# Moving the weight sums of a seven-product matrix multiplication into accumulating transfers, and scaling its inputs once

## The chip, the cores and the metric

The kernel runs on one NeuronCore of a Trainium2 chip. Its engines work from their own in-order queues: PE (TensorE, matrix multiplication), DVE (VectorE) and ACT (ScalarE) for element-wise work, POOL (GpSimd) for slower element-wise work, SP (SyncE), which here issues most DMA transfers. Sixteen DMA engines move the data. The metric is the time of one execution on the device in microseconds; lower is better. Three runs of the kernel before took 2226.47 to 2231.89 us, with a median of 2231.1.

## The reference, cut to what matters

One layer of a streaming encoder over 512 positions and 2048 channels, in float32. The change lies in its second half, the convolutional feed-forward block:

```
h    = rms_norm(x, pre_ffn_g)                      # x: 512 x 2048
up   = causal_depthwise_conv(h @ w_up, conv_w)     # w_up: 2048 x 11264, conv of 3 taps
gate, val = split(up, 2)                           # 5632 channels each
f    = (gelu(gate) * val) @ w_down                 # w_down: 5632 x 2048
x    = x + rms_norm(f, post_ffn_g)
```

The norm's factor (called r2 below) is one number per position, so it can be multiplied to h before the matrix product or to the product after it.

## The kernel before, in words

Tensors lie transposed: channels on the 128 partitions, the 512 positions along the free dimension. For precision each float32 operand of a matrix product is split into a high part (ACT, a cast to float32r) and the rest (DVE, a subtraction); a product is three matmuls, high x high, high x low, low x high. For weights ACT's cast `wh` is on L787 and DVE's subtraction `wl` on L788 (L100 and L101 in the plain products).

The 44 blocks of 128 hidden channels (`f`) each have a gate half and a val half. The first NP = 4 blocks are computed in the plain way by `up(0)` and `up(1)`, two blocks each, with `gemm`. The other 40 are the rows that this text speaks of: the loop `for f in range(NP, NFF)`. In a row, the 2 x 2 block product of weights (gate/val x lower/upper half of the input channels: w11, w12, w21, w22) and inputs (input-channel halves x position halves: q11, q12, q21, q22) is formed with seven products of half size instead of eight, from sums of weight blocks and sums of input quarters. Each `product` is 24 matmuls of 256 columns on one PSUM tile. Order on PE in a row: w11 x "11"; then, by `quad_end`, the last two products of the previous row (w22 x "t4", w12 x "22"); then s1 x "t1", s1 x "t2", w12 x "21", and w21 x "t3". The products of "t3" read on the trace as matmuls with `t2h`, those of "t1" and "t2" with `t0h` and `t1h`, or the like, by tile number.

Before the rows, the sums of the input quarters are made (`xsum`, L757) and split (`xsplit`, L761 and L762) from h without r2, so every result of a row has to be multiplied by r2 afterwards: GpSimd does that on L819 (val) and L823 (gate). Of the weights, `quad_load` fetches all four blocks (L801 to L810) with SP's queue, and GpSimd makes w21 + w22 into s1 (L805) and w11 - w21 into w21's buffer (L808). DVE makes the two other sums in the row, s1 - w11 (L841) and w12 - s1 (L848). DVE also combines the products in PSUM into gate and val (L818, L822, L845, L853, L854). `gated` then does the three taps of the convolution (first tap ACT on L726, two DVE on L728), ACT's gelu (L731), the product of gate and val (GpSimd, L732), and SP stores the block in DRAM (`fscr`, L733).

After the rows `down` multiplies the hidden blocks by w_down, four blocks at a time. `fload` loads four stored blocks (L876) and splits them (ACT L878, DVE L880).

The program states priorities (`tc.high_priority`: WPRI for weights, EPRI for what leaves PSUM), and a scheduler writes each engine's order from them before the run. A tile has a number of buffers; a load into one waits until the last reader of its former content is through. Tiles of a closed pool pass their place on: the pool `sp` of the rows (weight sums, `rb`, and a third pair of split buffers) is opened after `s16` is closed, which held the input quarters `yo`, and `hid`, of `down`, after the rows' `xt`.

## Time and profile before

| what | value |
|---|---|
| runs | 2226.47, 2231.1, 2231.89 us (median 2231.1) |
| profiled execution, its own time | 2227.7 us |
| its span, first to last instruction | 2225.9 us |
| mean granted TensorE clock | 0.966 of full speed |
| rows (40) | about 770 to 1704 us of the span |
| `down` | from about 1718 us on |

A busy share is an engine's busy time over the span. Matmuls are pipelined: one is shown for 0.28 us while the next starts 0.12 us later, so starts are what to count. A line such as "L845 DVE TENSOR_TENSOR ab<-mm,ab" is line 845 of the kernel, its engine, its operation, and the tiles it writes and reads. What stands in brackets behind "idle before" is how long the engine waited and for whom. "wl<-rb", "wl<-wraw" and "wl<-s" are the same subtraction on weights from different buffers.

### The profile page before, as it was taken

To read this page: it belongs to the slowest core of one execution; us is meant where nothing else is said; L and a number is where in the kernel's file an instruction comes from. 1 tells how busy PE (TensorE), PEld (TensorE's weight loads), DVE (VectorE), ACT (ScalarE), POOL (GpSimd) and SP (SyncE) were. 2 spreads that over 40 slices of the span, in tenths; PEclk is the share of its full clock that TensorE was granted. 3 is DMA by queue.
4 is the path that set the end of the run, shared out by engine and by line. 5 is a ranking of instruction groups with operands and counts; after the bars stand their busy time and mean duration, and the time that the engine had idled before them with its cause. 6 is when DMAs were issued, how large, how long until landed. Compare 5 with 4: busy or idle time off the path is not lost.

```text
span 2225.9 us, 30245 instructions
## 1 busy us (share of the span) xinstructions
PE 1997.7 (90%) x12070; PEld 1761.6 (79%) x12070; DVE 1688.0 (76%) x1893; ACT 811.2 (36%) x1047; POOL 725.6 (33%) x493
## 2 busy tenths in 40 slices
PE   7777988999987999989898998989987999999995
PEld 6565876777876789888898898988886888888884
DVE  5398999996459688988988889888886355555545
ACT  5112234334555433443433444334334422222223
POOL 7564145212123344435444444454441000000004
PEclk9888998999999999999999999999998999999998
DMA  5765665222423323233232332322225333433322
GB/s 198 190 207 178 186 206 164 95 95 85 171 99 119 127 101 106 94 111 103 89 116 95 102 110 88 119 96 100 105 95 194 123 114 119 135 116 114 104 95 95
DMA packets 124077, 275.88 MB, mean 124 GB/s; under 512 B 29472, under 2 KB 50976, under 8 KB 123424
## 3 DMA queue, kind: packets, MB, share of 16 engines
q1 hardware_dynamic: 119184, 271.85, 37.0%
q10 hardware_dynamic: 4752, 2.11, 0.4%
q8 instruction: 94, 1.54, 0.3%
q14 instruction: 47, 0.39, 0.1%
HBM read 241.21 MB, written 32.70 MB: 123 GB/s over the span
## 4 chain that ended last, share of the span: by engine, by line
PE 37%; DVE 20%; issue 7%; ACT 3%; DMA 0%; ACTq 0%; DVEq 0%; SPq 0%
PE mm L120 8%; PE mm L122 8%; PE mm L121 8%; DVE wl L788 7%; PE mm L793 5%; PE mm L794 4%; PE mm L795 4%; DVE s L841 4%; ACT wh L787 3%; DVE tmp L728 3%; DVE wraw L848 3%; DVE ab L822 1%; DVE ab L845 1%; DMA fin<-fscr 0%; DVE fa L920 0%
## 5 line engine op out<-in xcount | busy, mean ns | idle before, releaser
L101 DVE TENSOR_TENSOR wl<-wraw,wh 128x1024 fp32r<-128x1024 f32 (+1 forms) x193 | 254.6, 1320 | 245.5 <-ACT wh L100 239.5
L100 ACT CAST wh<-wraw 128x1024 fp32r<-128x1024 f32 (+1 forms) x193 | 201.6, 1046 | 508.8 <-PE mm L121 458.3
L122 PE MATMUL mm<-hl,wl 128*128 128x512 f32 x832 | 316.0, 412 | 64.5 <-DVE wl L101 64.5
L793 PE MATMUL mm<-hl,wh 128*128 128x256 f32 x1280 | 366.1, 286 | 5.7 <-ACT wh L787 5.1
L795 PE MATMUL mm<-hl,wl 128*128 128x256 f32 x1280 | 362.2, 283 | 0.0
L794 PE MATMUL mm<-hl,wh 128*128 128x256 f32 x1280 | 362.1, 283 | 0.0
L120 PE MATMUL mm<-hl,wh 128*128 128x512 f32 x832 | 333.6, 405 | 20.6 <-ACT wh L100 12.5
L121 PE MATMUL mm<-hl,wh 128*128 128x512 f32 x832 | 332.7, 402 | 0.2 <-DVE hl L691 0.2
L120 PE MATMUL mm<-hidh,wh 128*128 128x512 f32 x704 | 274.9, 391 | 14.4 <-ACT hidh L878 14.4
L121 PE MATMUL mm<-hidl,wh 128*128 128x512 f32 x704 | 274.6, 390 | 0.0
L122 PE MATMUL mm<-hidh,wl 128*128 128x512 f32 x704 | 258.1, 390 | 0.0
L793 PEld LDWEIGHTS mm<-hl,wh 128*128 128x128 f32 x1280 | 245.6, 192 | 10.8 <-ACT wh L787 7.3
L122 PEld LDWEIGHTS mm<-hl,wl 128*128 128x128 f32 x832 | 164.4, 198 | 111.2 <-DVE wl L101 76.1
L795 PEld LDWEIGHTS mm<-hl,wl 128*128 128x128 f32 x1280 | 245.8, 192 | 0.0
L794 PEld LDWEIGHTS mm<-hl,wh 128*128 128x128 f32 x1280 | 245.7, 192 | 0.0
L788 DVE TENSOR_TENSOR wl<-s,wh 128x1024 fp32r<-128x1024 f32 x80 | 162.2, 2028 | 89.1 <-ACT wh L787 89.1
L120 PEld LDWEIGHTS mm<-hl,wh 128*128 128x128 f32 x832 | 163.1, 196 | 57.3 <-ACT wh L100 14.2
L788 DVE TENSOR_TENSOR wl<-wraw,wh 128x1024 fp32r<-128x1024 f32 x120 | 194.4, 1620 | 7.4 <-ACT wh L787 4.6
L121 PEld LDWEIGHTS mm<-hl,wh 128*128 128x128 f32 x832 | 162.3, 195 | 36.4 <-DVE hl L691 1.2
L787 ACT CAST wh<-s 128x1024 fp32r<-128x1024 f32 x80 | 83.8, 1048 | 281.0 <-DVE s L841 169.1
L805 POOL TENSOR_TENSOR s<-rb 128x1024 f32<-128x1024 f32 x40 | 106.1, 2653 | 231.1 <-DMA rb<-in_ffn_w_quad 231.1
L571 DVE SCALAR_TENSOR_TENSOR csb<-z,c_conv_w,csb 128x512 f32<-128x512 f32 x210 | 178.8, 907 | 2.0 <-ACT csb L564 1.9
(262 smaller groups left out, 4111.9 us busy)
## 6 DMA issues: line engine op xcount, KB each, us to landing
wraw<-in_ffn_w_down SPq DMA_DIRECT2D x88, 512.0 KB, 3.2
wraw<-in_ffn_w_quad SPq DMA_DIRECT2D x80, 512.0 KB, 3.3
rb<-in_ffn_w_quad SPq DMA_DIRECT2D x80, 512.0 KB, 3.3
wraw<-in_w_in SPq DMA_DIRECT2D x47, 512.0 KB, 4.7
wraw<-in_w_out SPq DMA_DIRECT2D x32, 512.0 KB, 3.2
fscr<-tmp SPq DMA_DIRECT2D x44, 256.0 KB, 2.0
fin<-fscr SPq DMA_DIRECT2D x44, 256.0 KB, 3.8
cst<-cscr SPq DMA_DIRECT2D x16, 576.0 KB, 4.2
```

The lines of the kernel that those rows point to most:

```text
L100: se.copy(out=h[:, o], in_=raw[:, o])
L101: ve.tensor_tensor(out=l[:, o], in0=raw[:, o], in1=h[:, o].bitcast(F32), op=SUB)
L120: pe.matmul(ps[m], wh[:, kk, m, :], xh, start=k == 0, stop=False)
L121: pe.matmul(ps[m], wh[:, kk, m, :], xl, start=False, stop=False)
L122: pe.matmul(ps[m], wl[:, kk, m, :], xh, start=False, stop=k == nk - 1)
L571: ve.scalar_tensor_tensor(out=csb[:, c, :], in0=zk, scalar=w, in1=csb[:, c, :], op0=MUL, op1=ADD)
L787: se.copy(out=h, in_=raw)
L788: ve.tensor_tensor(out=l, in0=raw, in1=h.bitcast(F32), op=SUB)
L793: pe.matmul(o, h[:, k, :], xh_[:, k, :], start=first and k == 0, stop=False, skip_group_check=True)
L794: pe.matmul(o, h[:, k, :], xl_[:, k, :], start=False, stop=False, skip_group_check=True)
L795: pe.matmul(o, l[:, k, :], xh_[:, k, :], start=False, stop=last and k == 7, skip_group_check=True)
L805: ge.tensor_tensor(out=s1, in0=w21, in1=w22, op=ADD)
```

## The change: what it does

Four things, in the rows and around them.

The input quarters are multiplied by r2 once, in place, after up(0); the sums are then of scaled quarters, and all seven inputs are split anew: "t1", "t2", "t3" before up(1), and "11", "21", "t4", "22" after it in program order. The products need no r2 afterwards, so L819 and L823 go. "22" is split with its sign changed, and signs change in the sums that follow.

s1 is made by a load of w21 and an accumulating transfer that adds w22 to it in place, and a new s3 by a load of w11 and an accumulating transfer that adds w21. Both accumulating transfers are issued by GpSimd. w11, w12 and w22 are loaded as before, so a row has five plain loads and two accumulating ones. `rb` has two buffers instead of four, s3 has two.

The product of gate and val moves from GpSimd to DVE. In the first row the product w11 x "11" goes behind the two with s1.

Before the last `quad_end`, the first four hidden blocks are loaded from DRAM into tiles that are free by then (`evt`, `um`), and `fload(0)` uses these.

```diff
--- before.py
+++ after.py
@@ -717,7 +717,7 @@
         na[0] += 1
         return t
 
-    def gated(f, ab, mul):
+    def gated(f, ab):
         cvt = []
         for j in range(2):
             c = f + NFF * j
@@ -729,7 +729,7 @@
                                         op0=MUL, op1=ADD)
             cvt.append(o)
         se.activation(out=cvt[0], in_=cvt[0], func=AF.Gelu_apprx_tanh)
-        mul.tensor_tensor(out=cvt[0], in0=cvt[0], in1=cvt[1], op=MUL)
+        ve.tensor_tensor(out=cvt[0], in0=cvt[0], in1=cvt[1], op=MUL)
         sy.dma_start(out=fscr[:, f, :], in_=cvt[0])
 
     def up(i):
@@ -741,11 +741,16 @@
                 ve.tensor_tensor(out=t[:, 2:], in0=ps[j], in1=r2, op=MUL)
             ab.append(t)
         for f in range(2):
-            gated(2 * i + f, ab[2 * f:2 * f + 2], ge)
+            gated(2 * i + f, ab[2 * f:2 * f + 2])
 
     up(0)
 
 
+    for i in range(2):
+        for j in range(2):
+            o = slice(HS * j, HS * j + HS)
+            ve.tensor_tensor(out=yo[i][:, :, o], in0=yo[i][:, :, o],
+                             in1=r2[:, o].unsqueeze(1).broadcast_to([P, 8, HS]), op=MUL)
     q11, q12 = yo[0][:, :, 0:HS], yo[0][:, :, HS:S]
     q21, q22 = yo[1][:, :, 0:HS], yo[1][:, :, HS:S]
     xset = {"11": (hh[0][:, :, 0:HS], hl_[0][:, :, 0:HS]), "21": (hh[1][:, :, 0:HS], hl_[1][:, :, 0:HS]),
@@ -753,24 +758,33 @@
     for i in range(3):
         xset[f"t{i + 1}"] = tuple(tset[i])
 
-    def xsum(name, dst, in0, in1):
+    def xsum(dst, in0, in1):
         ve.tensor_tensor(out=dst, in0=in0, in1=in1, op=SUB)
 
-    def xsplit(name, src):
+    def xsplit(name, src, sign=1.0):
         h, l = xset[name]
-        se.copy(out=h, in_=src)
-        ve.tensor_tensor(out=l, in0=src, in1=h.bitcast(F32), op=SUB)
-
-    xsum("t1", q11, q12, q11)
-    xsplit("t1", q11)
-    xsum("t3", q12, q22, q12)
-    xsum("t2", q22, q22, q11)
-    xsplit("t2", q22)
+        if sign > 0:
+            se.copy(out=h, in_=src)
+            ve.tensor_tensor(out=l, in0=src, in1=h.bitcast(F32), op=SUB)
+        else:
+            se.activation(out=h, in_=src, func=AF.Copy, scale=-1.0)
+            ve.scalar_tensor_tensor(out=l, in0=src, scalar=-1.0, in1=h.bitcast(F32), op0=MUL, op1=SUB)
+
+
+    xsum(q12, q12, q11)
+    xsplit("t1", q12)
+    xsum(q12, q22, q12)
+    xsplit("t2", q12)
+    xsum(q12, q11, q12)
     xsplit("t3", q12)
-    xsum("t4", q21, q21, q22)
+    xsum(q12, q12, q11)
+    ve.tensor_tensor(out=q12, in0=q12, in1=q21, op=ADD)
     for i in range(1, NP // 2):
         up(i)
-    xsplit("t4", q21)
+    xsplit("11", q11)
+    xsplit("21", q21)
+    xsplit("t4", q12)
+    xsplit("22", q22, -1.0)
     s16x.close()
 
 
@@ -797,62 +811,71 @@
     def quad_load(f):
         src = a["ffn_w_quad"][f - NP]
         with tc.high_priority(offset=WPRI):
-            w21 = sp.tile([P, 1024], F32, name="rb", bufs=4)
-            sy.dma_start(out=w21, in_=src[2])
-            w22 = sp.tile([P, 1024], F32, name="rb", bufs=4)
-            sy.dma_start(out=w22, in_=src[3])
             s1 = sp.tile([P, 1024], F32, name="s1", bufs=2)
-            ge.tensor_tensor(out=s1, in0=w21, in1=w22, op=ADD)
+            sy.dma_start(out=s1, in_=src[2])
+            s3 = sp.tile([P, 1024], F32, name="s3", bufs=2)
+            sy.dma_start(out=s3, in_=src[0])
             w11 = wp.tile([P, 1024], F32, name="wraw", bufs=3)
             sy.dma_start(out=w11, in_=src[0])
-            ge.tensor_tensor(out=w21, in0=w11, in1=w21, op=SUB)
+            ge.dma_start(out=s1, in_=src[3], accum_op=ADD)
+            ge.dma_start(out=s3, in_=src[2], accum_op=ADD)
             w12 = wp.tile([P, 1024], F32, name="wraw", bufs=3)
             sy.dma_start(out=w12, in_=src[1])
-        return w11, w12, w21, w22, s1
+            w22 = sp.tile([P, 1024], F32, name="rb", bufs=2)
+            sy.dma_start(out=w22, in_=src[3])
+        return w11, w12, s3, w22, s1
 
     def quad_end(f, st_):
-        (w11, w12, w21, w22, s1), ab, (px, py, pz) = st_
+        (w11, w12, s3, w22, s1), ab, (px, py, pz) = st_
         gate, val = ab
         product(w22, "t4", py, False, True)
         with tc.high_priority(offset=EPRI):
-            ve.tensor_tensor(out=val[:, 2:2 + HS], in0=py[:, 0:HS], in1=val[:, 2:2 + HS], op=ADD)
-            ge.tensor_tensor(out=val[:, 2:], in0=val[:, 2:], in1=r2, op=MUL)
+            ve.tensor_tensor(out=val[:, 2:2 + HS], in0=py[:, 0:HS], in1=val[:, 2:2 + HS], op=SUB)
         product(w12, "22", pz, False, True)
         with tc.high_priority(offset=EPRI):
-            ve.tensor_tensor(out=gate[:, 2 + HS:], in0=pz[:, 0:HS], in1=gate[:, 2 + HS:], op=ADD)
-            ge.tensor_tensor(out=gate[:, 2:], in0=gate[:, 2:], in1=r2, op=MUL)
-        gated(f, ab, ge)
+            ve.scalar_tensor_tensor(out=gate[:, 2 + HS:], in0=pz[:, 0:HS], scalar=-1.0, in1=gate[:, 2 + HS:],
+                                    op0=MUL, op1=SUB)
+        gated(f, ab)
 
     before = None
     for f in range(NP, NFF):
         ws = quad_load(f)
-        w11, w12, w21, w22, s1 = ws
+        w11, w12, s3, w22, s1 = ws
         ab = [anext(), anext()]
         gate, val = ab
-        px = psm.tile([P, S], F32, name="mm")
-        product(w11, "11", px, True, False)
-        with tc.high_priority(offset=EPRI):
-            se.copy(out=val[:, 2:2 + HS], in_=px[:, 0:HS])
+        px, pz, py = (psm.tile([P, S], F32, name="mm") for _ in range(3))
+
+        def p1():
+            product(w11, "11", px, True, False)
+            with tc.high_priority(offset=EPRI):
+                se.copy(out=val[:, 2:2 + HS], in_=px[:, 0:HS])
+
         if before:
+            p1()
             quad_end(f - 1, before)
-        pz = psm.tile([P, S], F32, name="mm")
         product(s1, "t1", pz, True, False)
         with tc.high_priority(offset=WPRI):
-            ve.tensor_tensor(out=s1, in0=s1, in1=w11, op=SUB)
-        py = psm.tile([P, S], F32, name="mm")
+            ve.tensor_tensor(out=s1, in0=s1, in1=w11, op=ADD)
         product(s1, "t2", py, True, False)
+        if not before:
+            p1()
         with tc.high_priority(offset=EPRI):
-            ve.tensor_tensor(out=gate[:, 2 + HS:], in0=py[:, 0:HS], in1=val[:, 2:2 + HS], op=ADD)
+            ve.tensor_tensor(out=gate[:, 2 + HS:], in0=py[:, 0:HS], in1=val[:, 2:2 + HS], op=SUB)
         product(w12, "21", px, False, True)
         with tc.high_priority(offset=WPRI):
-            ve.tensor_tensor(out=w12, in0=w12, in1=s1, op=SUB)
+            ve.tensor_tensor(out=w12, in0=w12, in1=s1, op=ADD)
         with tc.high_priority(offset=EPRI):
             se.copy(out=gate[:, 2:2 + HS], in_=px[:, 0:HS])
-        product(w21, "t3", py, False, False)
+        product(s3, "t3", py, False, False)
         with tc.high_priority(offset=EPRI):
-            ve.tensor_tensor(out=val[:, 2 + HS:], in0=py[:, 0:HS], in1=val[:, 2:2 + HS], op=ADD)
+            ve.tensor_tensor(out=val[:, 2 + HS:], in0=py[:, 0:HS], in1=val[:, 2:2 + HS], op=SUB)
             ve.tensor_tensor(out=val[:, 2 + HS:], in0=pz[:, 0:HS], in1=val[:, 2 + HS:], op=ADD)
         before = (ws, ab, (px, py, pz))
+    f0 = []
+    for i in range(4):
+        t = evt() if i < 2 else t1.tile([P, S], F32, name="um", bufs=2)
+        sy.dma_start(out=t, in_=fscr[:, i, :])
+        f0.append(t)
     quad_end(NFF - 1, before)
     spx.close()
     upx.close()
@@ -872,8 +895,11 @@
     def fload(b):
         r = []
         for i in range(4):
-            t = hid.tile([P, S], F32, name="fin", bufs=6)
-            sy.dma_start(out=t, in_=fscr[:, 4 * b + i, :])
+            if b:
+                t = hid.tile([P, S], F32, name="fin", bufs=6)
+                sy.dma_start(out=t, in_=fscr[:, 4 * b + i, :])
+            else:
+                t = f0[i]
             h = hid.tile([P, S], F32R, name="hidh")
             se.copy(out=h, in_=t)
             l = hid.tile([P, S], F32R, name="hidl")
```

## Rows read from the trace of the kernel before

**Rows 1.** The page, part 1: busy us, share of the span, instructions.
```profile
PE 1997.7 (90%) x12070; PEld 1761.6 (79%) x12070; DVE 1688.0 (76%) x1893; ACT 811.2 (36%) x1047; POOL 725.6 (33%) x493
```

**Rows 2.** Stretches: busy us (instructions) per engine, PEclk, DMA share, GB/s.
```profile
800.00:1690.00 890.00, 806.44 (x6400) 782.40 (x6401) 789.40 (x688) 357.00 (x459) 394.89 (x189) 0.99 0.30 101
1650.01:1673.68 23.67, 21.10 (x168) 20.38 (x168) 21.22 (x19) 9.32 (x12) 9.97 (x6) 1.00 0.30 99
1673.68:1693.72 20.04, 20.04 (x167) 20.00 (x167) 17.19 (x19) 8.34 (x10) 3.58 (x4) 1.00 0.19 66
```

**Rows 3.** PE timeline, one t3 start: start us, duration us, instruction, idle before.
```profile
1673.68 0.38 PE L793 MATMUL mm<-t2h,wh 128*128 128x256 f32 x1 [1.44 <-DVE ab L845]
```

**Rows 4.** Single lines of DVE: xcount, ns min/median/max, first and last start.
```profile
L845 DVE TENSOR_TENSOR ab<-mm,ab x40: 409/411/424, 783.5 to 1693.2; 128x256 f32<-128x256 f32 x40
...
L841 DVE TENSOR_TENSOR s<-s,wraw x40: 1212/3308/3415, 775.3 to 1681.7; 128x1024 f32<-128x1024 f32 x40
```

**Rows 5.** Waits, 800 to 1690 us: total us, times, longest us.
```profile
PE mm L793 <- DVE ab L845: 54.3, 38, 1.5
```

**Rows 6.** DVE groups, 800 to 1690 us: busy us, mean ns, idle before.
```profile
L788 DVE TENSOR_TENSOR wl<-wraw,wh 128x1024 fp32r<-128x1024 f32 x115 | 187.4, 1630 | 3.2 <-ACT wh L787 0.4
...
L788 DVE TENSOR_TENSOR wl<-s,wh 128x1024 fp32r<-128x1024 f32 x76 | 155.4, 2045 | 86.5 <-ACT wh L787 86.5
...
L728 DVE SCALAR_TENSOR_TENSOR tmp<-ab,c_ffn_conv_w,tmp 128x512 f32<-128x512 f32 x153 | 107.4, 740 | 0.0
...
L788 DVE TENSOR_TENSOR wl<-rb,wh 128x1024 fp32r<-128x1024 f32 x76 | 92.1, 1212 | 0.0
...
L848 DVE TENSOR_TENSOR wraw<-wraw,s 128x1024 f32<-128x1024 f32 x39 | 77.2, 1980 | 1.4
...
L822 DVE TENSOR_TENSOR ab<-mm,ab 128x256 f32<-128x256 f32 x39 | 16.0, 411 | 0.0
```

**Rows 7.** Timeline of DVE and POOL around 1048 us.
```profile
1048.34 3.12 DVE L788 TENSOR_TENSOR wl<-s,wh 128x1024 fp32r<-128x1024 f32 x1 [1.41 <-ACT wh L787]
...
1047.97 2.40 POOL L805 TENSOR_TENSOR s<-rb 128x1024 f32<-128x1024 f32 x1 [5.36 <-DMA rb<-in_ffn_w_quad]
1050.44 3.27 POOL L808 TENSOR_TENSOR rb<-wraw,rb 128x1024 f32<-128x1024 f32 x1
```

**Rows 8.** A 512-column subtraction, line L880.
```profile
L880 DVE TENSOR_TENSOR hidl<-fin,hidh x44: 682/685/693, 1717.8 to 2114.4; 128x512 fp32r<-128x512 f32 x44
```

**Rows 9.** DMA: queue in 800 to 1690 us, issues (us to landing), slowest group.
```profile
q1 hardware_dynamic: 27087, 88.63, 29.1%
...
rb<-in_ffn_w_quad SPq DMA_DIRECT2D x74, 512.0 KB, 3.3
...
csb<-wscr SPq DMA_DIRECT2D x8, 256.0 KB, 8.8
```

**Rows 10.** Timelines at the start of the rows.
```profile
679.39 3.35 DVE L757 TENSOR_TENSOR s<-s 128x2048 f32<-128x2048 f32 x1
...
749.33 2.29 DVE L762 TENSOR_TENSOR hl<-s,hl 128x2048 fp32r<-128x2048 f32 x1 [0.59 <-ACT hl L761]
...
722.77 0.80 PE L122 MATMUL mm<-hl,wl 128*128 128x512 f32 x1 [4.77 <-DVE wl L101]
...
727.30 0.58 ACT L152 COPY rr<-aux 128x512 f32<-128x512 f32 x1 [9.88 <-PE aux L148]
...
751.65 0.33 SPq L801 DMA_DIRECT2D rb<-in_ffn_w_quad  x1
...
767.99 0.39 PE L122 MATMUL mm<-hl,wl 128*128 128x512 f32 x1
```

**Rows 11.** The end of the rows: timelines of PE and SP; a stretch.
```profile
1717.79 2.08 PE L120 MATMUL mm<-hidh,wh 128*128 128x512 f32 x4 [14.38 <-ACT hidh L878]
...
1700.45 1.01 SPq L915 DMA_DIRECT2D hl<-x1scr  x2
...
1720.00:1725.00 5.00, 5.00 (x18) 3.93 (x17) 3.37 (x5) 2.79 (x5) 0.00 (x0) 0.73 0.91 310
```

## The prediction

> **What bounds the kernel now.** I read the busy shares first, then a window over the rows, then who waits for whom there, then single rows. The page has PE busy for 90% and DVE for 76% of a span of 2225.9 us [rows 1], an average over stages with different limits. The part that the change edits most is the loop over 40 feed-forward rows. In the window from 800 to 1690 us DVE is busy for 789.4 of 890 us (89%) and PE for 806.4 [rows 2]: two engines near full, so each is often late for the other. A row's last own product (t3) starts behind the DVE instruction of L845 [rows 3], and L845 runs from 783.5 to 1693.2 us in 39 steps [rows 4], which is 23.33 us a row. Inside that, PE has 7 products of 24 matmuls, which took 20.04 us in the one row that has no gap [rows 2]. The rest is PE waiting, first of all 54.3 us for L845 [rows 5], 38 times 1.4.
>
> Why DVE is late can be read from its durations. The same 128x1024 instruction takes 1.21 us on average in one group and 1.63, 2.05 and 1.98 us in the others [rows 6]; L841 alone ranges from 1.21 to 3.42 us, with a median of 3.31 [rows 4]. The timeline shows when: at 1048.34 DVE starts one of 3.12 us, while GpSimd runs its additions from 1047.97 to 1053.7 [rows 7]. The last row, from t3 to t3 the third stretch of its group, shows the other side: nothing is loaded for a further row, GpSimd is busy for 3.58 us instead of 9.97, DVE for 17.19 instead of 21.22, and the row takes 20.04 us instead of 23.67, with PE busy all through [rows 2].
>
> **The change, part by part.**
>
> *GpSimd's arithmetic goes.* Removed are two 128x1024 sums, two multiplications by r2 and the gate product a row. DVE's row then holds nine 128x1024 instructions at 1.21 us (10.9), four taps at 0.74 (3.0), five 256-column PSUM instructions at 0.42 (2.1), all from [rows 6], and the gate product, which is new there: 0.69, as the 512-column two-input subtraction of L880 [rows 8]. Sum 16.7 us, against 789.4 x 23.33 / 890 = 20.7 now. The form of L822 with a negation is counted at the same 0.42; at the taps' 0.74 it would add 0.3, still under PE's 20. So DVE stops being the limit, and what is late next is PE itself. The floor is the 20.04 us of the last row, the ceiling (nothing gained) 23.33. I take 20.3, near the floor: the last row still had the r2 products, but an in-order DVE now carries one instruction more. Gain 39 x (23.33 - 20.3) = 118 us, bounds 0 and 128.
>
> *Two accumulating transfers.* Per row there are five plain loads instead of four, and two accumulations of 512 KB from GpSimd's queue. That queue holds nothing else in the rows, so behind an accumulation that waits for its first load stands only the next accumulation. No accumulating transfer is in this trace. Plain loads land after 3.3 us, and the transfers use 29.1% of the 16 engines [rows 9]: 0.291 x 23.33 = 6.8 us a row for four loads and a 256 KB store, 1.5 for each 512 KB. Five loads and the store make 8.3; with two accumulations of A each, a row costs 8.3 + 2A of transfer time. At A = 1.5 (as a load) that is 11.3; at 3 (the old value is read as well) 14.3; the far end is the slowest group of the trace, 256 KB landing after 8.8 us [rows 9], so 17.6 for 512 KB and 43 us a row. Break-even with 23.33 is A = 7.5. I take 3, as the added work is one more read of the same bytes. In latency, 3.3 us for the load and some 5 for the accumulation lie before the sum can be cast. The sums are made about a row ahead (the one at 1047.97 [rows 7] serves the next row) and s1 and s3 have two buffers each, so this hides; without that cover it would stand in every row.
>
> The Trainium skill (SBUF — State Buffer, section "SBUF: two separate sides") speaks against transfers from GpSimd's queue: while DVE runs an instruction that takes both ports, GpSimd cannot write the descriptors. By that rule two-input instructions such as those of [rows 6] do not block them, and a row stays at 20.3; if they did, the sums would come late and the third rival's price would be due. No run here shows it yet.
>
> *The start of the rows.* Before, the sums and three splits of the input quarters ran on DVE during up(0), 2.29 us for a split and up to 3.35 for a sum [rows 10]; they held up PE, which waited 4.77 us for a weight half at 722.77 [rows 10]. Now they stand behind r2, which ACT delivers by 727.9 [rows 10]. Without them up(0) ends some 5 us earlier, r2 is there at 723, and up(1), which ended at 768.2 [rows 10], ends at 763. But from r2 on DVE holds 4 scalings, 5 sums and 5 splits that can run at once (14 x 2.29 = 32 us), up(0)'s evacuation, taps and gate products (four and two instructions of 0.69 and eight taps of 0.74, 10 us) and eight weight halves (10): 52 us in the 42 us of up(1). Behind up(1) come two more splits (4.6) and its own evacuation (10), then seven 128x1024 instructions of the first row (9): 723 + 52 + 15 + 9 = 799 for the first t3, against 783.9 now (L845's 783.5 and its 0.4 [rows 4]). The first s1 load can be late too: the first load for sums was issued at 751.65, just when the t4 split ended (749.33 + 2.29) [rows 10], so its buffer seems to lie where the quarters lay. In series, 790 + 3.3 + 5 + 2.3 us and four products of 2.9 give 812. Bounds -7 (early up(1), no stop in the first row) and +28; I take +14.
>
> *The end of the rows.* PE started down(0) at 1717.79, after 14.38 us for ACT's cast of the reloaded hidden tiles [rows 11]. Their loads had queued behind two 2 MB transfers issued at 1700.45, and from 1720 to 1725 the transfer engines were still 91% busy and the granted clock stood at 0.73 [rows 11], part of it at the lower of its two levels, 1.2 GHz. With four tiles read before the last products, this wait and some 2 us of slow clock go. What is late next is down(0)'s third weight tile, behind the same 4 MB: some 3 us. Gain 13, bounds 0 and 17.
>
> *Costed at nothing:* the sign changes (same counts of instructions) and ACT, which casts for three more splits, once, and is busy for 357 of 890 us [rows 2]; PE covers both. Uncovered, ACT's casts would cost some 7 us if each takes as long as DVE's half of a split.
>
> **Sum.** The profiled execution took 2227.7 us (1.8 around its span). 2227.7 - 118 + 14 - 13 = 2111. The median of the runs is 3.4 higher, which I leave to the range.
>
> **The rivals.**
> 1. *DVE's order stays the limit.* L845 stands in its queue behind a weight half, the w12 sum and taps, and PE stopped 1.44 us for it in a contended row [rows 3]. If that order keeps the stop, a row is 20.04 + 1.5 = 21.5: gain 39 x 1.83 = 71, total 2227.7 - 71 + 14 - 13 = 2158. For: DVE gets a product more. Against: in the last row the stop was gone.
> 2. *The start is free, or dear.* By its bounds the total is 2090 or 2125.
> 3. *The accumulations are the bound.* For each, the 16 engines or GpSimd's issue take A, in every row. It decides from A = 7.5. At A = 10 a row is 28.3, 39 x 5 = 195 us more: 2227.7 + 195 + 1 = 2424, slower. For: nothing in the trace prices them. Against: A would have to be five loads.
> 4. *The change doesn't do what it says:* issuing from GpSimd stretches DVE as the sums did. With half the contention left, half of the rows' gain goes: 2170. For: two issues a row remain there. Against: the sums took 2.40 + 3.27 us [rows 7], and an issue reads no tile.
>
> **How the numbers follow.** The forecast with any start has 0.65, rival 1 0.15, rival 4 0.07, rival 3 above break-even 0.10, and 0.03 an accumulation that eats just the gain. The likeliest case's own range is 2090 to 2130; the range reaches to 2172 for rivals 1 and 4 and leaves out the slow side. A difference of over 0.3% (6.7 us) is what can be told from no change here. Faster 0.87, same 0.03, slower 0.10.
>
> **What would show it.** Right: t3 products 20.0 to 20.6 us apart, DVE's 128x1024 instructions all near 1.21 us, no PE wait for L845, DVE busy for some 0.82 of a row, transfers at a share of 0.5 to 0.75, the first t3 product near 799, a wait of a few us before down(0). Wrong: DVE's durations still split between 1.2 and 2 to 3 us (rival 4); ACT's cast of s1 or s3 waiting for a transfer in each row (rival 3); a stop of over a microsecond at each t3 (rival 1).

## The result, and the profile after

The changed kernel takes 2112.34 us (median of 4 runs, 2112.06 to 2115.38) against 2230.6 for the kernel before in the same comparison: a ratio of 0.9476, 95% interval 0.946 to 0.9492. The forecast was 2111, in a range from 2085 to 2172.

The code is longer, so lines have new numbers: the release of t3 is L863 (it was L845), the combination after t3 L871 (L853), s1 + w11 L858 (L841), w12 + s1 L866 (L848), the splits of weights L802 (L788) behind ACT's casts L801, matmuls L807 to L809. L732, the gate product, is on DVE; L820 and L821 are the accumulations; L904 casts the hidden tiles (L878).

The page, part 1, of the changed kernel answers to [rows 1]:

```profile
PE 1962.2 (93%) x12070; PEld 1750.8 (83%) x12070; DVE 1518.5 (72%) x1945; ACT 829.3 (39%) x1050; POOL 364.9 (17%) x369
```

A window over 770 us of the rows answers to [rows 2] (busy us and instructions by engine, PEclk, DMA share, GB/s), then the release of t3 and s1 + w11 as single lines, which answer to [rows 4]:

```profile
820.00:1590.00 770.00, 770.00 (x6419) 770.00 (x6418) 606.86 (x728) 369.85 (x459) 64.04 (x74) 1.00 0.69 192
```

```profile
L863 DVE TENSOR_TENSOR ab<-mm,ab x40: 416/418/425, 801.1 to 1587.9; 128x256 f32<-128x256 f32 x40
...
L858 DVE TENSOR_TENSOR s<-s,wraw x40: 1224/1225/1226, 787.8 to 1577.3; 128x1024 f32<-128x1024 f32 x40
```

PE is busy in all 770 us, and the list of its waits has no entry there; before it had 54.3 us for the release of t3 [rows 5]. The release now comes every (1587.9 - 801.1) / 39 = 20.17 us. s1 + w11 took up to 3.42 us in [rows 4]; now all forty take 1.224 to 1.226. The DVE groups of the same window (busy us, mean ns of one, idle before), which answer to [rows 6], show the same of all long instructions:

```profile
L802 DVE TENSOR_TENSOR wl<-s,wh 128x1024 fp32r<-128x1024 f32 x115 | 140.7, 1223 | 86.6 <-ACT wh L801 86.6
L802 DVE TENSOR_TENSOR wl<-wraw,wh 128x1024 fp32r<-128x1024 f32 x114 | 139.3, 1222 | 24.3 <-ACT wh L801 21.4
...
L802 DVE TENSOR_TENSOR wl<-rb,wh 128x1024 fp32r<-128x1024 f32 x39 | 47.8, 1226 | 16.1 <-ACT wh L801 16.1
...
L732 DVE TENSOR_TENSOR tmp<-tmp 128x512 f32<-128x512 f32 x39 | 26.7, 685 | 0.0
```

The DMA view of that window (queues with their share of 16 engines; issues with the median us to landing) answers to [rows 9]. Queue q0 holds GpSimd's accumulations:

```profile
q1 hardware_dynamic: 32387, 107.96, 39.5%
q0 software_dynamic: 10656, 38.80, 29.5%
...
s<-in_ffn_w_quad POOLq DMA_DIRECT2D x74, 512.0 KB, 7.7
```

**Where the time went.** The span fell by 113.4 us, 2225.9 to 2112.5. The first and the last release of t3 cut it into three parts:

| part | before | after | change | forecast |
|---|---|---|---|---|
| up to the first release | 783.5 | 801.1 | +17.6 | +14 |
| 39 rows | 909.7 | 786.8 | -122.9 | -118 |
| from the last release on | 532.7 | 524.6 | -8.1 | -13 |

At the start PE waits longest in 690 to 830 us for a cast of the first row. The waits of PE there, and below them the timelines around it (start us, us, engine, line, idle before and its releaser). The second block is one line of the kernel before, the reciprocal on the way to r2; the third, of the changed kernel, begins with the same reciprocal:

```profile
PE mm L807 <- ACT wh L801: 24.8, 2, 23.8
PE mm L122 <- DVE wl L101: 6.4, 2, 5.2
```

```profile
722.64 0.16 DVE L142 RECIPROCAL rs<-rs 128x4 f32<-128x4 f32 x1
```

```profile
705.10 0.18 DVE L142 RECIPROCAL rs<-rs 128x4 f32<-128x4 f32 x1 [0.27 <-ACT rs L141]
...
710.96 0.59 ACT L152 COPY rr<-aux 128x512 f32<-128x512 f32 x1 [4.81 <-PE aux L148]
...
769.20 2.28 DVE L771 SCALAR_TENSOR_TENSOR hl<-s,hl 128x2048 fp32r<-128x2048 f32 x1
...
771.51 0.33 SPq L815 DMA_DIRECT2D s<-in_ffn_w_quad  x1
...
775.77 1.05 POOL L820 DMA_DIRECT2D s<-in_ffn_w_quad  x1 [72.56 <-DMA s<-in_ffn_w_quad]
...
785.47 1.05 ACT L801 CAST wh<-s 128x1024 fp32r<-128x1024 f32 x1 [8.94 <-DMA s<-in_ffn_w_quad]
```

This is a series: the last split of an input quarter ends at 771.48, the first s1 load starts at 771.51 in the room it leaves, the accumulation is issued at 775.77, and the cast of the sum starts at 785.47.

At the end PE waits 5.4 us ahead of the last projection, where it waited 14.38 [rows 11]. ACT's timeline shows what stands there: the casts of the four tiles loaded early are in its queue behind the first taps and the gelu of the last block. The loads themselves are long done (SP issues them at 740.77 and 787.49 us). Two windows of 5 us show the granted clock in and after that stop at 0.75 and 0.57, partly at the lower of the two levels, 1.2 GHz, while the DMA engines are full; a third shows it back at 1.00, with 24 matmuls where there were 15:

```profile
1599.74 1.33 ACT L726 ACTIVATE tmp<-ab,c_ffn_conv_w 128x512 f32<-128x512 f32 x2
1603.11 0.63 ACT L731 ACTIVATE tmp<-tmp 128x512 f32<-128x512 f32 x1 [2.04 <-DVE tmp L728]
1603.64 1.12 ACT L904 CAST hidh<-evt 128x512 fp32r<-128x512 f32 x2
```

```profile
1600.00:1605.00 5.00, 0.70 (x2) 0.61 (x3) 4.90 (x7) 2.96 (x6) 0.00 (x0) 0.75 1.01 424
1605.00:1610.00 5.00, 5.00 (x15) 3.89 (x14) 1.94 (x4) 0.81 (x2) 0.00 (x0) 0.57 0.97 365
1610.00:1615.00 5.00, 5.00 (x24) 4.14 (x23) 1.70 (x2) 2.78 (x5) 0.00 (x0) 1.00 0.95 354
```

### The profile page after: what moved, and what is told of

The parts are those of the page before. It is cut to its first block, busy times and chain, and to the rows that moved or that the text cites. A ratio compares the mean times of both kernels' runs of the same rounds, so it can differ in the third digit from the quotient of the medians.

```text
span 2112.5 us, 30280 instructions
## 1 busy us (share of the span) xinstructions
PE 1962.2 (93%) x12070; PEld 1750.8 (83%) x12070; DVE 1518.5 (72%) x1945; ACT 829.3 (39%) x1050; POOL 364.9 (17%) x369
## 5 line engine op out<-in xcount | busy, mean ns | idle before, releaser
L807 PE MATMUL mm<-hl,wh 128*128 128x256 f32 x1280 | 362.5, 283 | 1.6 <-ACT wh L801 1.0
L809 PE MATMUL mm<-hl,wl 128*128 128x256 f32 x1280 | 362.1, 283 | 0.0
L807 PEld LDWEIGHTS mm<-hl,wh 128*128 128x128 f32 x1280 | 245.9, 192 | 2.0 <-ACT wh L801 1.2
L809 PEld LDWEIGHTS mm<-hl,wl 128*128 128x128 f32 x1280 | 245.8, 192 | 0.0
L802 DVE TENSOR_TENSOR wl<-s,wh 128x1024 fp32r<-128x1024 f32 x120 | 146.8, 1223 | 100.5 <-ACT wh L801 100.5
L801 ACT CAST wh<-s 128x1024 fp32r<-128x1024 f32 x120 | 126.2, 1051 | 191.4 <-DVE s L858 92.0
L801 ACT CAST wh<-wraw 128x1024 fp32r<-128x1024 f32 x120 | 126.2, 1052 | 184.4 <-PE mm L808 184.4
L802 DVE TENSOR_TENSOR wl<-wraw,wh 128x1024 fp32r<-128x1024 f32 x120 | 146.7, 1222 | 28.2 <-ACT wh L801 25.2
```

The costliest lines, as they stand in the source:

```text
L801: se.copy(out=h, in_=raw)
L802: ve.tensor_tensor(out=l, in0=raw, in1=h.bitcast(F32), op=SUB)
L807: pe.matmul(o, h[:, k, :], xh_[:, k, :], start=first and k == 0, stop=False, skip_group_check=True)
L809: pe.matmul(o, l[:, k, :], xh_[:, k, :], start=False, stop=last and k == 7, skip_group_check=True)
```

## The experiments

All ratios are to the kernel before on the same chip; brackets hold the ratio and its 95% interval. In experiments 1, 2 and 7 "theory A" is the prediction's: GpSimd's two-input instructions stretched DVE's, and a stretched DVE held up PE. In the others each expectation says what its theory A is. Three dots in a code block stand for lines left out.

### 1. The sums back on GpSimd

```diff
...
+            s3 = sp.tile([P, 1024], F32, name="rb", bufs=4)
+            sy.dma_start(out=s3, in_=src[2])
...
-            sy.dma_start(out=s1, in_=src[2])
...
+            ge.tensor_tensor(out=s1, in0=s3, in1=w22, op=ADD)
...
-            ge.dma_start(out=s1, in_=src[3], accum_op=ADD)
-            ge.dma_start(out=s3, in_=src[2], accum_op=ADD)
+            ge.tensor_tensor(out=s3, in0=w11, in1=s3, op=ADD)
...
```

With the accumulations one plain load a row goes, and `rb` has its four buffers again.

> The changed kernel with one part undone: GpSimd makes the two weight sums again (two-input additions of 1024 columns), everything else as changed (inputs scaled once, gate product on DVE, early hidden tiles). Theory A, GpSimd's two-input reads stretch DVE's instructions and so the row: DVE's 1024-column instructions go from 1.22 back to 1.6 to 3.2 us, GpSimd is busy 5.7 us a row, a row takes 21.5 to 23.3 us, the total 2160 to 2230. Rival B, the row was shortened by taking the r2 and gate products off GpSimd (their waits stood in the chain from DVE to ACT's taps): the row stays at 20.2 to 20.5, the total 2105 to 2125.

Measured: 2186.06 us (0.9813, 0.9785 to 0.9842). DVE groups, 830 to 1580 us, then PE's waits there:

```profile
L802 DVE TENSOR_TENSOR wl<-s,wh 128x1024 fp32r<-128x1024 f32 x68 | 139.9, 2058 | 79.0 <-ACT wh L801 79.0
...
L857 DVE TENSOR_TENSOR s<-s,wraw 128x1024 f32<-128x1024 f32 x33 | 109.2, 3308 | 1.1
```

```profile
PE mm L807 <- DVE ab L862: 24.2, 34, 0.7
PE mm L809 <- DVE wl L802: 22.7, 30, 0.8
```

The release of t3 comes every 22.13 us. Two GpSimd instructions a row bring back 39 x 1.96 = 76 us: the wait for DVE stands in every row again, though the two products with r2 and the gate product stay away from GpSimd.

The timelines also show what the stretch is. One pair of sums, and the two DVE instructions beside it:

```profile
1200.25 2.40 POOL L819 TENSOR_TENSOR s<-rb 128x1024 f32<-128x1024 f32 x1 [14.18 <-DMA rb<-in_ffn_w_quad]
1202.97 3.02 POOL L822 TENSOR_TENSOR rb<-wraw,rb 128x1024 f32<-128x1024 f32 x1 [0.32 <-DMA wraw<-in_ffn_w_quad]
...
1200.76 2.97 DVE L802 TENSOR_TENSOR wl<-s,wh 128x1024 fp32r<-128x1024 f32 x1 [1.46 <-ACT wh L801]
1203.77 3.31 DVE L857 TENSOR_TENSOR s<-s,wraw 128x1024 f32<-128x1024 f32 x1
```

The sums end at 1202.65 and 1205.99, DVE's instructions at 1203.73 and 1207.08: 1.08 and 1.09 us later. Wherever in 840 to 1580 us such a sum ends inside a 128x1024 DVE instruction of over 1.4 us, here and in the kernel before, DVE's instruction ends 1.07 to 1.10 us after it. So DVE does not run slower beside a sum: it waits until the sum has ended and needs most of its 1.22 us from there.

### 2. Three products a row back on GpSimd, the sums still transfers

```diff
-        ve.tensor_tensor(out=cvt[0], in0=cvt[0], in1=cvt[1], op=MUL)
+        ge.tensor_tensor(out=cvt[0], in0=cvt[0], in1=cvt[1], op=MUL)
...
+            ge.tensor_tensor(out=val[:, 2:], in0=val[:, 2:], in1=r2, op=MUL)
...
+            ge.tensor_tensor(out=gate[:, 2:], in0=gate[:, 2:], in1=r2, op=MUL)
```

> The changed kernel with the other part undone: GpSimd multiplies gate and val by r2 (once more, so the result is scaled twice) and makes the gate product in every block, while the weight sums stay transfers. Theory A: GpSimd is busy about 4 us a row with 512-column products, as in the last row of the kernel before, which took 20.04; the row is 20.1 to 20.6 us, the total 2110 to 2130. Rival B: the row goes above 21.5 us, the total above 2160.

Measured: 2111.49 us (0.9478, 0.9451 to 0.9506), nothing lost. The window of 830 to 1580 us:

```profile
830.00:1580.00 750.00, 750.00 (x6253) 750.00 (x6252) 645.96 (x670) 359.20 (x446) 204.65 (x185) 1.00 0.69 193
```

DVE is stretched here too (the group of splits from `wraw` takes 1573 ns in the mean, the split of w22 2009) and is busy for 86% of the window, as in experiment 1 (654.73 of 750, 87%). PE never waits, and a row takes 20.19 us. So taking the sums off GpSimd brings the whole gain even with the products left there: 23.33 to 20.19. Taking the products off alone, which is what experiment 1 is against the kernel before, brings 1.20 of it, 23.33 to 22.13. And DVE's busy share doesn't tell a row that loses from one that doesn't.

### 3. Own room for the first row's sums

The first row's s1 and s3 go into four free tiles of 512 columns, loaded and accumulated in halves, in place of the room that the input quarters leave.

```diff
...
+                if two == "s1":
+                    t = [evt() for _ in range(2)]
+                else:
+                    t = [t1.tile([P, S], F32, name="um", bufs=2) for _ in range(2)]
...
```

> The changed kernel, but the first row's s1 and s3 lie in four 512-column tiles that are free since the first half of the layer, so that their loads need not wait for the input quarters' place. Theory A, the first row is late because the first load of s1 waits for the split of quarter 22 (23.8 us of PE waiting for ACT's cast of s1): the wait goes down to 0 to 5 us, the DVE instruction that releases the first t3 product moves from 801.1 to 779 to 786 us, the total is 2090 to 2098. Rival B, DVE's backlog of scalings, sums and splits behind r2 sets the first row anyway: it stays at 795 or later, the total above 2105.

Measured: 2097.32 us (0.9415, 0.9388 to 0.9442), the lowest median of this study. The release of t3 as a single line:

```profile
L884 DVE TENSOR_TENSOR ab<-mm,ab x40: 415/420/428, 783.8 to 1570.5; 128x256 f32<-128x256 f32 x40
```

The first release is 17.3 us earlier than in the changed kernel and the rest is unchanged. Of these, 2.8 us stand already at r2 (708.8 against 711.6), ahead of the series; the other 14.5, most of the loss at the start, were the series of load and accumulation. The longest wait of PE there is now 5.2 us, for a weight half behind the four scalings.

### 4. The hidden tiles loaded late again

```diff
-    f0 = []
-    for i in range(4):
-        ...
-        sy.dma_start(out=t, in_=fscr[:, i, :])
```

> The changed kernel without the early loads of the first four hidden blocks; they are loaded after the rows, as before. Theory A, these loads queue behind the two 2 MB loads of x: PE's wait before down(0) goes from 5.4 to 13 to 15 us, with about 1 us more of slow clock, the total is 2119 to 2124. Rival B, the wait has become short because the rows end differently: it stays at 5 to 6 us, the total 2112.

Measured: 2122.25 us (0.9527, 0.9499 to 0.9554). PE's wait ahead of the last projection:

```profile
PE mm L120 <- ACT hidh L896: 14.1, 1, 14.1
```

14.1 us instead of 5.4, and the span is 7.6 us longer: the early loads are worth what the end gained (8.1).

### 5. Every accumulation twice

```diff
+            ge.dma_start(out=s1, in_=src[3], accum_op=ADD)
+            ge.dma_start(out=s3, in_=src[2], accum_op=ADD)
```

> The changed kernel with each accumulating transfer issued twice, the second behind the first (so s1 and s3 hold the added block twice). In the trace of the changed kernel the software queue takes 29.5% of the 16 engines for two accumulations in 20.17 us, about 3 us each, and the other queue 39.5%, 8.0 us a row. Theory A, transfers have room for what the change added and the sums come a row ahead: four accumulations make 8 + 12 = 20 us of transfer time a row, the share goes to 0.93 to 1, and a row is 20.2 to 22 us, total 2110 to 2190, still under the kernel before. Rival B, accumulations are late already: ACT's casts of s1 wait for transfers in each row and a row is over 24 us, total above 2260.

Measured: 2124.92 us (0.954, 0.9497 to 0.9582). The window of 830 to 1580 us, the accumulations' queue there, and the release of t3:

```profile
830.00:1580.00 750.00, 750.00 (x6253) 750.00 (x6251) 590.87 (x709) 359.27 (x447) 128.05 (x148) 1.00 0.96 247
```

```profile
q0 software_dynamic: 21312, 77.60, 55.2%
```

```profile
L865 DVE TENSOR_TENSOR ab<-mm,ab x40: 407/416/423, 811.5 to 1598.3; 128x256 f32<-128x256 f32 x40
```

The transfers use 96% of the DMA engines, and a row still takes 20.17 us without a wait of PE. All of the 10 us by which the span is longer (2122.5 against 2112.5) are at the start, where the series has one accumulation more (first release at 811.5 against 801.1). An accumulation costs 0.552 x 20.17 / 4 = 2.8 us of all engines, 0.295 x 20.17 / 2 = 3.0 in the changed kernel.

### 6. The sums of experiment 1, held back

```diff
+            if before:
+                ge.tensor_copy(out=mark, in_=before[1][0][:, 2 + HS:3 + HS])
...
+            ge.tensor_tensor(out=s1, in0=s3, in1=w22, op=ADD)
```

> As the run with the two sums on GpSimd again (22.13 us a row), but GpSimd starts them only after DVE's combination of gate in the row before (a one-column copy of gate stands ahead of them in its queue), so they stretch other DVE instructions: those between the t3 product and the first cast of s1, not the chain cast, split of s1, s1 + w11, cast. Theory A1, it is the place of the contention in DVE's chain that counts: the stretch of s1's split and of s1 + w11 goes, a row is 20.2 to 21.2 us, total 2110 to 2150. Rival A2, the amount of stretching alone counts: a row stays at 21.8 to 22.5, total 2170 to 2200. Rival C: the later sum makes the cast of s1 late: above 22.5.

Measured: 2184.2 us (0.9806, 0.976 to 0.9851). The time lies in the range of A2, but the run tells nothing on the question. Nothing tied the sums to the copy, and GpSimd's queue holds them ahead of the copy of their own row: in its timeline the first sum starts at 1199.78, while DVE's split of s1 starts at 1200.26 and takes 3.00 us; in experiment 1 the pair starts at 1200.25 and 1200.76. The same two instructions were stretched.

### 7. Reads or writes of GpSimd beside the accumulations

On a spare tile, behind each row's second accumulation: four additions of 512 columns, or ten memsets.

```diff
+            for _ in range(4):
+                with tc.issue_after(last):
+                    last = ge.tensor_tensor(out=dummy, in0=dummy, in1=dummy, op=ADD).ins
```

```diff
+            for _ in range(10):
+                with tc.issue_after(last):
+                    last = ge.memset(dummy, 0.0).ins
```

> The changed kernel with four more GpSimd additions of 512 columns a row (on a spare tile, both inputs in SBUF), right behind the issue of the second accumulation. Theory A: DVE's two-input instructions that run beside them go from 1.22 to 1.5 us and more (means of the groups up to 2), as beside the sums; the row is 20.2 to 22.

> As the run with four more GpSimd additions, but ten memsets of the same spare tile instead, which only write. Theory A (reads of GpSimd hold up DVE's second input, writes don't): DVE's 1024-column instructions stay at 1.21 to 1.25 us and the row at 20.2, total 2109 to 2116. Rival B (any GpSimd work on SBUF does): the means go up as beside the additions.

Measured, one run each: 2111.32 and 2108.91 us. DVE groups of 830 to 1580 us, first with the additions, then with the memsets:

```profile
L802 DVE TENSOR_TENSOR wl<-s,wh 128x1024 fp32r<-128x1024 f32 x112 | 150.8, 1346 | 74.5 <-ACT wh L801 74.5
...
L864 DVE TENSOR_TENSOR s<-s,wraw 128x1024 f32<-128x1024 f32 x38 | 73.3, 1928 | 1.3
```

```profile
L802 DVE TENSOR_TENSOR wl<-s,wh 128x1024 fp32r<-128x1024 f32 x111 | 135.7, 1223 | 84.3 <-ACT wh L801 84.3
...
L864 DVE TENSOR_TENSOR s<-s,wraw 128x1024 f32<-128x1024 f32 x37 | 45.3, 1225 | 1.3
```

GpSimd is busy for 280.09 us of the window with the additions and for 251.87 with the memsets; only the additions stretch DVE (1.93 us instead of 1.225). So it is GpSimd's reading that collides, not its being busy; additions read two inputs and memsets none, and reading one was not tried. Neither costs time, as there is slack in the row.

### 8. The sums bound to a later place

What experiment 6 meant to do, with a real dependence.

```diff
             s1 = sp.tile([P, 1024], F32, name="s1", bufs=2)
...
+            if before:
+                ge.tensor_copy(out=s1[:, 0:1], in_=before[0][4][:, 0:1])
+            ge.tensor_tensor(out=s1, in0=s3, in1=w22, op=ADD)
```

> Two of four sums on GpSimd again, as in the run where they go back to it (22.13 us a row, 2186 us), but each row's first sum may only start after the s1+w11 addition of the row before: one column of that row's s1 is copied into the new tile first, so the order is a real dependence. In the run that tried this with a copy to a separate column, nothing tied the sums to the copy, and they stood beside the same two VectorE instructions as before: the split of s1 (3.00 us) and s1+w11 (3.32 us), which lie on one chain (split t1, s1+w11, cast, split t2). Theory A1, a stretched VectorE instruction costs time only where it lies on that chain: the sums now stand beside the splits of 21 and t3, w12+s1 and the taps, which run one or two products ahead of TensorE; split of s1 and s1+w11 near 1.22 us, row 20.2 to 20.8 us, 2112 to 2140 us in all. Theory A2, the amount of VectorE's busy time decides wherever it lies: row near 22 us, 2170 to 2200.

Measured: 2171.65 us (0.975, 0.9737 to 0.9763), 21.82 us a row. PE's wait in 830 to 1580 us, and one row of DVE's timeline from the combination after t3 to the next one:

```profile
PE mm L807 <- DVE ab L864: 49.0, 34, 1.6
```

```profile
1193.78 0.43 DVE L872 TENSOR_TENSOR ab<-mm,ab 128x256 f32<-128x256 f32 x1 [0.36 <-PE mm L809]
...
1198.68 1.22 DVE L859 TENSOR_TENSOR s<-s,wraw 128x1024 f32<-128x1024 f32 x1
...
1201.11 2.69 DVE L802 TENSOR_TENSOR wl<-s,wh 128x1024 fp32r<-128x1024 f32 x1 [0.86 <-ACT wh L801]
...
1204.05 3.10 DVE L802 TENSOR_TENSOR wl<-wraw,wh 128x1024 fp32r<-128x1024 f32 x1
...
1211.99 0.41 DVE L864 TENSOR_TENSOR ab<-mm,ab 128x256 f32<-128x256 f32 x1
...
1215.63 0.42 DVE L872 TENSOR_TENSOR ab<-mm,ab 128x256 f32<-128x256 f32 x1 [0.36 <-PE mm L809]
```

The sums did move: s1 + w11 takes 1.22 us again, and the splits for t2 and for w12 x "21" take 2.69 and 3.10. The time hardly fell, and A1's forecast missed. The sums did not land where A1 wanted them, though: the split for t2 is the last of the four instructions of its chain. Still the chain alone doesn't give the time: the row is 1.65 us longer than PE's 20.17, and the split for t2 is stretched by 1.47. A2, the amount of DVE's work, fits this run.

### 9. Scalings cut as well, and casts of hidden tiles on GpSimd

Experiment 3 with its four scalings in pieces of two channels; and that kernel with the casts of the first four hidden tiles moved from ACT to GpSimd.

```diff
+            for k in range(0, 8, 2):
+                ve.tensor_tensor(out=yo[i][:, k:k + 2, o], in0=yo[i][:, k:k + 2, o],
+                                 in1=r2[:, o].unsqueeze(1).broadcast_to([P, 2, HS]), op=MUL)
```

```diff
+                ge.tensor_copy(out=h, in_=t)
```

> The kernel in which the first row's s1 and s3 have their own four tiles (2097.3 us), and besides the four scalings of the input quarters are cut into pieces of two channels. Theory A: the 6.3 us that TensorE waited for a split standing behind the uncut scalings fall to 2 or less; first release of t3 3 to 6 us earlier, rows unchanged at 20.17 us: 2091 to 2095 us. Rival: more instructions on VectorE and no shorter wait, since the block's length is the same and only its cutting differs and the order has the split behind all pieces: 2096 to 2099.

> As the kernel with both starts mended (first row's sums in own tiles, scalings cut), and the casts of the first four hidden tiles on GpSimd, which does nothing then, in place of ScalarE, where they stand behind the last block's taps and gelu. Theory A (the 5.4 us that TensorE waits ahead of the last projection is ScalarE's order, and that is what the end kept of the gain forecast): wait falls to 0 to 3 us, and the time by 2 to 5 us against that kernel: 2087 to 2092. Rival: the splits on VectorE of the same tiles stand behind the same taps and the product, so the wait turns into one for VectorE: same as that kernel within 1 us, or slower if GpSimd's cast is slow.

Measured: 2100.13 us (0.943, 0.9418 to 0.9443) and 2102.33 (0.9439, 0.9426 to 0.9451). Neither gains on experiment 3. Cutting took PE's wait for the weight half from 6.3 to 3.8 us, and its wait for the splits of the first row rose from 6.8 to 9.2. With the casts on GpSimd the wait ahead of the last projection changed its name and not its length:

```profile
PE mm L121 <- DVE hidl L932: 5.4, 1, 5.4
```

So it isn't ACT's order alone: DVE's splits of the same tiles stand behind the same block's taps and gate product. Both rivals were right in kind: the first gave 2096 to 2099, and the second kernel is 2.2 us slower than the first where it gave 1, or slower.

### 10. More work for DVE, nothing stretched

```diff
+            for _ in range(4):
+                with tc.issue_after(last):
+                    last = ve.tensor_tensor(out=dummy, in0=dummy, in1=dummy, op=ADD).ins
```

> The changed kernel, with four additions of 128x512 on a spare tile more on VectorE in each row, placed behind w12+s1; GpSimd still does no arithmetic, nothing is stretched, and the result is untouched. In the four runs where VectorE bounds the row, its busy time a row and the row's length differ by the same amount: before 20.67 of 23.33 us (2.66 left idle), sums on GpSimd 19.32 of 22.13 (2.81), sums held back 19.02 of 21.82 (2.80); in the changed kernel 15.87 of 20.17. Theory A2 (a row is the longer of TensorE's 20.17 us and VectorE's busy time plus 2.7 to 2.8 us that it can't fill, wherever the busy time lies): four additions at 0.685 us (the gate product's duration on tiles of this size) make 18.6 us busy, so 21.3 to 21.4 us a row, 39 steps of 1.15 to 1.25 us, 2157 to 2163 us. Theory A1 (only what lies on the chain split of t1, s1+w11, cast, split of t2 costs): none of the four stands there, 20.2 to 20.5 us a row, 2112 to 2126 us.

Measured: 2114.72 us (0.949, 0.9462 to 0.9519). The window of 830 to 1580 us, and DVE's timeline from the release to the combination after t3:

```profile
830.00:1580.00 750.00, 750.00 (x6252) 750.00 (x6252) 668.46 (x856) 359.80 (x448) 62.18 (x72) 1.00 0.71 194
```

```profile
1202.44 0.69 DVE L872 TENSOR_TENSOR evt<-evt 128x512 f32<-128x512 f32 x1
1203.04 0.42 DVE L866 TENSOR_TENSOR ab<-mm,ab 128x256 f32<-128x256 f32 x1
...
1205.17 0.69 DVE L872 TENSOR_TENSOR evt<-evt 128x512 f32<-128x512 f32 x1
...
1207.51 0.69 DVE L872 TENSOR_TENSOR evt<-evt 128x512 f32<-128x512 f32 x1
1208.11 0.42 DVE L877 TENSOR_TENSOR ab<-mm,ab 128x256 f32<-128x256 f32 x1
```

DVE is busy for 89%, as much as in the kernel before [rows 2], and PE doesn't wait once. A2 falls. The additions ran in gaps in which DVE had waited for casts or for PE (its idle time ahead of the splits of s1 and s3 fell from 86.6 to 53.3 us in such a window), and two of the four stand between release and combination, where PE runs t3 meanwhile.

**What the row's length follows.** Read side by side, the timelines give a loop. PE's t3 waits for the release; its result frees the combination; from there DVE works through its queue, in order, to the next release. If the stretch on DVE from the combination to the release, and the way back over PE, together exceed PE's 20.17 us, the loop sets the row. Starts of one row each, in us:

| kernel | combination to release | release to combination | sum | mean row | DVE busy |
|---|---|---|---|---|---|
| before | 19.84 | 3.64 | 23.48 | 23.33 | 89% |
| sums on GpSimd (1) | 18.67 | 3.65 | 22.32 | 22.13 | 87% |
| sums bound later (8) | 18.21 | 3.64 | 21.85 | 21.82 | 87% |
| products on GpSimd (2) | 16.37 | 3.79 | 20.16 | 20.19 | 86% |
| changed | 15.48 | 4.68 | 20.16 | 20.17 | 79% |
| more work on DVE (10) | 15.09 | 5.07 | 20.16 | 20.18 | 89% |

In experiments 1 and 8 the combination waits for PE in every row, and the way back is 3.64 us. In the last three lines it is longer, since the row then goes by PE's 20.17 us or the combination stands behind other work on DVE. The kernel before differs: there the combination waits for PE in 6 of 40 rows only, and in the others it follows straight on DVE's own splits, so that DVE's queue sets the way back too (3.83 us in the mean). The stretch is not all work: in it DVE waits for casts of ACT, 2.86 us in the changed kernel and 2.31 in experiment 1, and work that is added can fill such gaps, as in experiment 10.

So A1 was right that place decides, but the place is this whole stretch and not the four instructions I named: both instructions stretched in experiment 8 lie in it, and the split of w22 that GpSimd's gate product stretches in experiment 2 lies outside it. Experiment 2 is close to the limit: 16.37 + 3.64 is 0.16 under PE's 20.17. This form was made after the runs; it fits all six, and no run tested it with a number in advance.

## Why the prediction was right, point by point

The forecast of 2111 lies 1.3 us from the median of 2112.34. That it is so near is luck: the three parts were off by -4.9, +3.6 and +4.9 us, which partly cancel, and the profiled execution that they come from was the slowest of its four, at 2115.38.

**Rows: forecast -118, measured -122.9.** The mechanism is shown: experiment 1 undoes the sums alone and 1.96 us a row come back, with DVE's two long durations beside it. DVE's forecast row of 16.7 us was 606.86 x 20.17 / 770 = 15.9 (an instruction often starts some 0.08 us before the one ahead of it ends, which the sum of durations counts twice), the gate product 0.685 as taken from [rows 8], the instruction with a negation 0.42. The row of 20.17 lies midway between the value taken, 20.3, and the last row of before, 20.04, which was no floor after all. What the prediction did not separate: the two sums are enough for the whole gain. The three products that also left GpSimd cost nothing where the sums are transfers, and 1.20 us a row where they are not.

**Rival 1** (DVE's order keeps the stop) did not come, because the stretch before the release shrank by 4.4 us where 3.3 were needed (23.48 - 20.17). What is left is 20.17 - 15.48 - 3.64 = 1.05 us, and more where added work fills a gap.

**Accumulations: A = 3 taken, 3.0 measured** (2.8 in experiment 5). The break-even of 7.5 left them far from the bound, and even four a row, at a DMA share of 0.96, cost nothing in the rows. Landing took 7.7 us in the median instead of some 5, which the lead of a row hides: between 820 and 1590 us no cast of ACT waits for a transfer. Rival 3 is out.

**Issuing from GpSimd (rival 4).** DVE's instructions keep 1.22 us and an issue takes 0.87 (64.04 us by 74), so neither holds up the other. That agrees with the Trainium skill (SBUF — State Buffer, section "SBUF: two separate sides"): it has GpSimd locked out of writing descriptors by DVE instructions in a 2-port mode, and infers that two-input ones like these leave it free to write them. The same section says that the shared ports are locked against a two-input DVE instruction only by a GpSimd instruction that reads SBUF; experiment 7 agrees, with 1.93 us beside additions and 1.225 beside memsets.

**Start: forecast +14, measured +17.6, by another path.** Here the working was wrong though its sum came out near. The term that failed is r2 in DVE's queue (723 + 52 + 15 + 9 = 799), and the choice of that queue as what sets the first row. r2 came at 711.6, not at 723, since the sums and splits had also stood ahead of r2's own small steps on DVE (the reciprocal of L142 went from 722.64 to 705.10). From 711.6 the same count gives 788. In experiment 3, where no cast waits for a transfer, r2 comes at 708.8, the count gives 785, and the first release ends at 784.2. What set the start is the alternative that the prediction worked out and did not take: the loads find room only when the quarters are split, then load, accumulation, cast and products in series. I had 812 for it, with the splits ending at 790: they ended at 771.5, load and accumulation took 14 us to the cast at 785.5 and not 8.3, and the rest to the end of the release 16.1 and not 13.9.

**End: forecast -13, measured -8.1.** The early loads work (experiment 4), but I had next in line the third weight tile, some 3 us, and the 2 us of slow clock gone. No wait for that tile came. Instead PE waits 5.4 us for casts that stand behind the last block's taps and gelu, and the granted clock still falls to 0.57, where 15 matmuls start in 5 us instead of 24: that is 1.9 us lost. The mis-sized term is what ACT, and behind it DVE, do first. Experiment 9 shows that moving the casts alone doesn't help.

## What to carry to other kernels

When two engines are both near full, look for the loop between them: the in-order stretch on one engine from the instruction that the other frees to the one that frees the other. A stretched instruction costs time if it lies in that stretch and the loop is then longer than the row that the other engine needs; a busy share tells neither (89% cost 3.2 us a row in one kernel here and nothing in another). And when loads replace arithmetic, ask at the first iteration where their tiles lie: room that is freed late turned a hidden latency into some 15 us.

## What was not expected of the hardware

That an accumulating transfer of 512 KB takes 2.8 to 3.0 us of all sixteen DMA engines, against 1.45 for a plain load (0.395 x 20.17 by five loads and a store of half the size), was the guess; that at a share of 0.96 PE lost nothing was not expected. A stretched 128x1024 DVE instruction ended 1.07 to 1.10 us after the GpSimd sum that it stood beside. GpSimd's memsets stretched nothing on DVE; additions that kept GpSimd busy for about as long stretched one group of DVE's instructions by 57% in the mean (1.928 against 1.225 us).
